# Spare products of a projection stage in the general PSUM banks, in turn with the projections

## Chip, cores, metric

The kernel runs on one core of a Trainium2 chip. The metric is device time in microseconds (us) of one execution, the median of several runs. A second kernel, the change, computes the same thing with the same instructions in another order.

## What is computed

Two layers of a hybrid block work on 512 image tokens and 256 context tokens of width 1024. Cut to one layer:

```
h  = rms_norm(x) * (1 + scale) + shift          # also hc, of the context
(a_qkv, a_z, a_beta, a_alpha, b_q, b_kv, b_z, c_qkv, c_z, merge) = split(h @ w_in)
y_a = gated_head_rmsnorm(bidir_delta(short_conv(a_qkv), ...), a_z)   # 4 heads, chunks of 64
y_b = window_attention(b_q, b_kv, ...) * silu(b_z)
y_c = retention_out(bidir_retention(c_qkv), c_z)
out = (sigmoid(merge)[0] * (y_a @ w_br[0]) + sigmoid(merge)[1] * (y_b @ w_br[1])
       + sigmoid(merge)[2] * (y_c @ w_br[2])) @ w_o
x   = x + gate * out                            # context likewise, but not in the last layer
```

Branch A is a gated delta rule: in every chunk a unit lower triangular matrix is inverted (`triangular_solve` in the reference), then a chain of states runs over the chunks in both directions. Nothing of the `z` columns and of the `merge` columns is needed until the branches end.

## The kernel before

Every product with `w_in` is made in blocks of 128 columns, named by what they are: `aq0` to `aq3`, `ak0`.., `av0`.. are the projections of branch A, `az`, `bz`, `cz` the gates of the three branches, `m0_0` to `m2_7` the merge gates. A weight block is loaded (`wr`), cast by ScalarE to `wh` and its remainder taken by GpSimd as `wl`; `prod` (L305) then does 24 matmuls of 512 columns into a `px` bank for the image tokens and, in layer 0 only, 24 of 256 columns into a `pc` bank for the context (`hh`, `hl` are the two parts of `h`). PSUM has 2 `px` banks, 1 `pc` bank and 5 general ones (`pg`, `gps` at L252).

The A heads are worked in two pairs. For a pair, `delta_proj` makes six projections, each followed by a short convolution: one tap on ScalarE, the others as `scalar_tensor_tensor` on VectorE (L285), then turned to tokens by TensorE (`to_tok`, L602). `delta_mats` makes the chunk matrices with small matmuls in `pg` banks and VectorE's L285 and L288. `delta_inv` inverts the 32x32 blocks on VectorE: transposes (L733, L735), 62 short L288 operations, transposes back (L747, L748), then copies of the blocks on VectorE (L763) and ScalarE (L766, 12 of 32x192 elements). `levels` (L790) combines the blocks on TensorE; its first matmul waits for all copies. `delta_chain` is the chain over the chunks.

What nobody needs soon fills TensorE in the meantime: the generator `aside` (L1211) makes the spare products, the z and merge gates, one per step. ScalarE writes `tanh` of the bank into `kept` (L282 is the helper of every activation); for a z block VectorE also multiplies `kept` with the bank (L285), so that a z bank comes free only behind VectorE. Then ScalarE's queue stores `kept` in DRAM. `weave` at L1297 to L1302 sets the stages of a layer, and `FILL[l]` how many spare products stand in each: beside the projections of the second pair (with the matrices and inverse of the first), first chain, second pair's matrices, second inverse, second chain, each attention step, and ahead of the second token product `tokproj(w1)`. `BACK` says behind the how-many-last spare product the levels may begin on TensorE.

The order on each engine is fixed when the program is built: a scheduler with priorities (`hi`) sorts the instructions. An engine does them in that order, so a wait of one holds up all behind it.

```
        for nm in ms[0:6] + z("a") + ms[6:8] + z("b") + ms[8:12] + z("c") + ms[12:]:
            px, pc = self.pblk(l, nm, not last)
            self.asides.append(self.last)
```

Of the kernel before, what the change touches and what calls it, by code (L numbers as in the profile page):

```python
# [9 lines left out]
F32 = mybir.dt.float32  # L10
F32R = mybir.dt.float32r
BF16 = mybir.dt.bfloat16
AF = mybir.ActivationFunctionType
# [4 lines left out]
D, SEQ, CTX, DEPTH = 1024, 512, 256, 2  # L18
# [14 lines left out]
C1 = 3  # L33
AH = 2
BG = (0, 2)
FILL = ((5, 4, 2, 7, 5, 1, 1), (6, 3, 3, 9, 5, 1, 2))
BACK = ((2, 3), (2, 2))

NAMES = (["aq%d" % i for i in range(4)] + ["ak%d" % i for i in range(4)]
# [5 lines left out]
BLK = {n: i for i, n in enumerate(NAMES)}  # L45
# [117 lines left out]
class Builder:  # L163
# [142 lines left out]
    def prod(self, ps, w, acts, sl, ks=None):  # L306
        hi, lo = w
        n = len(acts)
        ks = ks or range(n)
        for k in ks:  # L310
            self.mm(ps, hi[k], acts[k][0].r[:, sl], start=(k == 0), stop=False)
            self.mm(ps, hi[k], acts[k][1].r[:, sl], start=False, stop=False)
        for k in ks:
            self.last = self.mm(ps, lo[k], acts[k][0].r[:, sl], start=False, stop=(k == n - 1)).ins.name

    def proj(self, dram, acts, ctx, w=None):
        w = w or self.weight(dram, len(acts))
        px = self.px.tile([128, 512], F32, name="px")
        self.prod(px, w, acts, slice(0, SEQ))
        pc = None  # L320
        if ctx:
            pc = self.pc.tile([128, 512], F32, name="pc")[:, 0:CTX]
            self.prod(pc, w, acts, slice(SEQ, TOK))
        return px, pc

# [27 lines left out]
                self.prod(ps[i], w, self.hs, PART[i], range(k0[i], k))  # L353
                k0[i] = k

    def pblk(self, l, name, ctx, w=None):
# [9 lines left out]
        return self.proj(self.a["wblk"][l, BLK[name]], self.hs, ctx, w)  # L366


    def ada_head(self):
# [347 lines left out]
    def delta_inv(self, st, back):  # L717
# [37 lines left out]
        for d in range(2):  # L755
            wsrc, tsrc = (Z, M) if d == 0 else (M, Z)

            own, other = (0, 2) if d == 0 else (3, 1)
            for hh, h in enumerate(st.heads):
                W[h, d] = self.alloc()  # L760
                nc.gpsimd.memset(W[h, d].f, 0.0)
                for q in range(4):
                    made.append(nc.vector.tensor_copy(blk(W[h, d], q), lane(wsrc, q, d, hh)))  # L763
                for q, t, c in ((own, Q, 32 * (own % 2)), (own + 1 - 2 * d, Q, 32 * (1 - own % 2)), (other, T, 0)):
                    made.append(self.act(six(t.f)[32 * q:32 * q + 32, hh, :, c:c + 32],
                                         lane(tsrc, q, d, hh), AF.Copy))  # L766
                yield
        self.free_inv()
        yield from self.levels(st, W, T, Q, made, self.asides[-back])
        self.free(T, Q, *st.U.values())  # L770

    def levels(self, st, W, T, Q, made, behind):
# [440 lines left out]
    def aside(self, l, last):  # L1213
        nc = self.nc
        n = SEQ if last else TOK
        self.kept = {}
        z = lambda b: ["%sz%d" % (b, i) for i in range(4)]
        ms = ["m%d_%d" % (r, d) for r in range(3) for d in range(8)]
        for nm in ms[0:6] + z("a") + ms[6:8] + z("b") + ms[8:12] + z("c") + ms[12:]:
            px, pc = self.pblk(l, nm, not last)  # L1220
            self.asides.append(self.last)
            t = self.fp.tile([128, TOK], F32, name="kept")
            for ps, sl in ((px, slice(0, SEQ)), (pc, slice(SEQ, TOK)))[:1 if last else 2]:
                self.act(t[:, sl], ps, AF.Tanh, scale=0.5)
                if nm[1] == "z":
                    self.stt(t[:, sl], t[:, sl], 1.0, ps, ALU.add, ALU.mult)
            g = self.dp.tile([128, n], F32, name="%s_%d" % (nm, l))
            nc.scalar.dma_start(g, t[:, 0:n])
            self.kept[nm] = g
            yield  # L1230
# [9 lines left out]
    def layer(self, l, xs, rs, mod, vec, row, ada):  # L1240
# [12 lines left out]
        self.asides = []  # L1253
        self.fill = self.aside(l, last)
        self.mods = self.ada(ada) if ada else iter(())
        F = FILL[l]
# [37 lines left out]
        self.delta_gates(l, ba, row)  # L1294
        for _ in p0:
            pass
        weave((seq(self.delta_mats(l, last, st[0]), self.delta_inv(st[0], BACK[l][0])), 45),  # L1297
              (self.delta_proj(l, 1, vec, last, st[1]), 6), fill(F[0]))
        weave((self.hi(self.delta_chain(l, last, st[0])), 6), fill(F[1]))
        weave((self.hi(self.delta_mats(l, last, st[1])), 4), fill(F[2]))  # L1300
        weave((self.hi(self.delta_inv(st[1], BACK[l][1])), 43), fill(F[3]))
# [157 lines left out]
def seq(*gens):  # L1459
    for g in gens:  # L1460
        yield from g


def weave(*tasks):

    live = [[0.0, i, g, n] for i, (g, n) in enumerate(tasks)]
    while live:
        t = min(live)
        try:
            next(t[2])  # L1470
            t[0] += 1.0 / t[3]
        except StopIteration:
            live.remove(t)
# [22 lines left out]
```

## Time and profile before

| what | value |
|---|---|
| median of 3 runs | 1822.45 us (1821.61 to 1828.53) |
| the profiled execution, its own time | 1822.54 us |
| its span | 1820.7 us |
| mean granted clock of TensorE | 0.978 |
| TensorE busy | 1716.5 us, 94% of the span |
| VectorE busy | 1051.9 us, 58% |
| ScalarE busy | 843.8 us, 46% |
| GpSimd busy | 591.9 us, 33% |

PE is TensorE, PEld its weight loads, DVE VectorE, ACT ScalarE, POOL GpSimd, SP SyncE. A row of a timeline gives the start, the duration, the engine, the line, the operation and the tiles it writes and reads; in square brackets at its end stands how long the engine was idle just before and what released it. A granted clock of 1.00 is 2.4 GHz, 0.5 is 1.2 GHz.

### The profile page before, as it was taken

Reading aid. Unit: us, or ns where it says so; the run is one execution under the profiler, and the core shown is the slowest. Engines: PE = TensorE matmul, PEld = TensorE weight load, DVE = VectorE, ACT = ScalarE, POOL = GpSimd, SP = SyncE. Lnnn points to the kernel's source line nnn. Section 1 sums busy time; section 2 is a strip of 40 time slices with the busy share of each in tenths; the row PEclk is TensorE's granted clock in tenths of the full one; section 3 lists DMA queues with packets and bytes.
Section 4 is the critical chain, followed back from the end, with each engine's and each line's share of the span. In section 5 each row is a group of like instructions: output and inputs, shape, how many; then the busy total and the mean of one; then the engine's idle time right before and its main releaser. Section 6 shows DMA issues by size and latency. Waiting matters only on the chain. (4 is left out here: it accounts for less than half of the span.)

```text
span 1820.7 us, 30653 instructions
## 1 busy us (share of the span) xinstructions
PE 1716.5 (94%) x11574; PEld 1457.0 (80%) x11574; DVE 1051.9 (58%) x2531; ACT 843.8 (46%) x2018; POOL 591.9 (33%) x739
## 2 busy tenths in 40 slices
PE   7999999899999999999999899889799999999997
PEld 4788888788877778988888688678688777888786
DVE  4668758732564553346563647957925657445653
ACT  6565546343544544222233556365444655433244
POOL 2322422312312214121453614432333322322553
PEclk9999999999999999999999899989999999999998
DMA  8211211322244233014453112212233332212542
GB/s 310 80 35 65 85 33 62 110 77 105 81 140 154 96 127 132 33 53 145 134 176 112 59 41 76 93 36 67 96 111 122 116 105 80 90 53 82 170 160 70
DMA packets 73748, 180.67 MB, mean 99 GB/s; under 512 B 8832, under 2 KB 16384, under 8 KB 73600
## 3 DMA queue, kind: packets, MB, share of 16 engines
q1 hardware_dynamic: 62144, 154.07, 26.1%
q10 hardware_dynamic: 11456, 24.65, 3.6%
q8 instruction: 91, 1.49, 0.3%
q14 instruction: 57, 0.47, 0.1%
HBM read 150.89 MB, written 27.79 MB: 98 GB/s over the span
## 5 line engine op out<-in xcount | busy, mean ns | idle before, releaser
L291 POOL TENSOR_TENSOR wl<-wr,wh 128x256 fp32r<-128x256 f32 x640 | 505.0, 818 | 1058.3 <-ACT wh L282 805.6
L261 PE MATMUL px<-hh,wh 128*128 128x512 f32 (+1 forms) x1088 | 433.8, 403 | 24.5 <-DVE kept L285 11.8
L261 PE MATMUL px<-hl,wh 128*128 128x512 f32 (+1 forms) x1088 | 431.9, 399 | 3.4 <-DVE hl L285 1.9
L261 PE MATMUL px<-hh,wl 128*128 128x512 f32 (+1 forms) x1088 | 286.9, 394 | 0.0
L282 ACT ACTIVATE wh<-wr 128x1024 fp32r<-128x1024 f32 (+1 forms) x184 | 174.3, 947 | 229.5 <-PE pc L261 109.3
L288 DVE TENSOR_TENSOR t<-t,t 128x512 f32<-128x512 f32 (+21 forms) x411 | 252.9, 616 | 42.3 <-ACT t L282 29.7
L261 PEld LDWEIGHTS px<-hh,wh 128*128 128x128 f32 x1088 | 209.3, 193 | 69.8 <-DVE kept L285 14.3
L282 ACT ACTIVATE t<-t 32x192 f32<-32x192 f32 (+10 forms) x314 | 168.2, 548 | 194.4 <-DVE t L285 124.6
L261 PEld LDWEIGHTS px<-hl,wh 128*128 128x128 f32 x1088 | 210.3, 193 | 44.1 <-DVE hl L285 6.8
L261 PE MATMUL pg<-t,t 128*128 128x128 f32 (+2 forms) x1616 | 231.3, 285 | 11.4 <-DVE t L288 11.0
L261 PEld LDWEIGHTS pg<-t,t 128*128 128x128 f32 x1616 | 206.6, 191 | 34.0 <-issue 11.6
L261 PEld LDWEIGHTS px<-hh,wl 128*128 128x128 f32 x1088 | 198.7, 191 | 37.6 <-issue 2.0
L261 PE MATMUL pc<-hh,wh 128*128 128x256 f32 x696 | 176.4, 288 | 9.9 <-DVE kept L285 5.7
L261 PE MATMUL pc<-hl,wh 128*128 128x256 f32 x696 | 177.6, 290 | 1.9 <-DVE hl L285 1.9
L261 PEld LDWEIGHTS pc<-hh,wh 128*128 128x128 f32 x696 | 134.4, 193 | 15.7 <-DVE kept L285 6.6
L261 PEld LDWEIGHTS pc<-hl,wh 128*128 128x128 f32 x696 | 134.9, 194 | 7.1 <-DVE hl L285 3.2
L282 ACT ACTIVATE t<-pg 128x128 f32<-128x128 f32 (+4 forms) x216 | 77.6, 383 | 109.7 <-PE pg L408 37.0
L261 PE MATMUL px<-t,wh 128*128 128x512 f32 x384 | 101.5, 402 | 4.2 <-DVE t L285 4.1
L261 PE MATMUL pc<-hh,wl 128*128 128x256 f32 x696 | 103.8, 289 | 0.0
L282 ACT ACTIVATE t<-px 128x128 f32<-128x128 f32 (+2 forms) x120 | 54.7, 465 | 101.8 <-PE px L261 94.6
L261 PEld LDWEIGHTS pc<-hh,wl 128*128 128x128 f32 x696 | 92.7, 196 | 0.9 <-issue 0.8
L261 PE MATMUL px<-t,hh 128*128 128x272 f32 (+1 forms) x384 | 86.6, 313 | 1.3 <-POOL t L291 1.0
(191 smaller groups left out, 2320.8 us busy)
## 6 DMA issues: line engine op xcount, KB each, us to landing
wr<-wblk SPq DMA_DIRECT2D x120, 512.0 KB, 3.3
t<-wada SPq DMA_DIRECT2D x48, 384.0 KB, 4.6
wr<-wbr SPq DMA_DIRECT2D x48, 256.0 KB, 2.7
m<-kept ACTq DMA_DIRECT2D x24, 384.0 KB, 2.3
t<-m SPq DMA_DIRECT2D x24, 384.0 KB, 3.6
wr<-wout SPq DMA_DIRECT2D x16, 512.0 KB, 3.3
t<-wada SPq DMA_DIRECT2D x24, 256.0 KB, 4.8
m<-kept ACTq DMA_DIRECT2D x24, 256.0 KB, 2.0
```

What stands on the lines that cost most here:

```text
L261: return self.nc.tensor.matmul(out, lhsT=lhsT, rhs=rhs, start=start, stop=stop)
L282: return self.nc.scalar.activation(out, in_, func, **k)
L288: self.nc.vector.tensor_tensor(out=out, in0=in0, in1=in1, op=op)
L291: self.nc.gpsimd.tensor_tensor(out=out, in0=in0, in1=in1, op=op)
```

## The change

It has four parts. The numbers of spare products per stage change (`FILL`). Their order changes: in layer 0 and 1 the first 5 and 6 are merge gates, then two `az`, then merge gates up to the second inverse, then the other two `az`, the `bz` and the `cz`; so the second pair's matrices and inverse have merge gates alone. In the projection stage (`self.behind`) a spare product takes `pg` banks, and a projection may be issued only behind the last spare product made so far, so that the two alternate on TensorE. In `delta_inv` ScalarE's copies are issued behind the tanh of an earlier spare product.

```
@@ -33,7 +33,7 @@
 C1 = 3
 AH = 2
 BG = (0, 2)
-FILL = ((5, 4, 2, 7, 5, 1, 1), (6, 3, 3, 9, 5, 1, 2))
+FILL = ((5, 2, 4, 7, 6, 1, 0), (6, 2, 4, 9, 6, 1, 1))
 BACK = ((2, 3), (2, 2))
 
 NAMES = (["aq%d" % i for i in range(4)] + ["ak%d" % i for i in range(4)]
@@ -311,15 +311,16 @@
             self.mm(ps, hi[k], acts[k][0].r[:, sl], start=(k == 0), stop=False)
             self.mm(ps, hi[k], acts[k][1].r[:, sl], start=False, stop=False)
         for k in ks:
-            self.last = self.mm(ps, lo[k], acts[k][0].r[:, sl], start=False, stop=(k == n - 1)).ins.name
-
-    def proj(self, dram, acts, ctx, w=None):
+            self.end = self.mm(ps, lo[k], acts[k][0].r[:, sl], start=False, stop=(k == n - 1)).ins
+            self.last = self.end.name
+
+    def proj(self, dram, acts, ctx, w=None, other=False):
         w = w or self.weight(dram, len(acts))
-        px = self.px.tile([128, 512], F32, name="px")
+        px = self.gps() if other else self.px.tile([128, 512], F32, name="px")
         self.prod(px, w, acts, slice(0, SEQ))
         pc = None
         if ctx:
-            pc = self.pc.tile([128, 512], F32, name="pc")[:, 0:CTX]
+            pc = self.gps(CTX) if other else self.pc.tile([128, 512], F32, name="pc")[:, 0:CTX]
             self.prod(pc, w, acts, slice(SEQ, TOK))
         return px, pc
 
@@ -353,7 +354,7 @@
                 self.prod(ps[i], w, self.hs, PART[i], range(k0[i], k))
                 k0[i] = k
 
-    def pblk(self, l, name, ctx, w=None):
+    def pblk(self, l, name, ctx, w=None, other=False):
         if l == 0 and name in self.begun:
             b = self.begun[name]
             self.advance(b, KB)
@@ -363,7 +364,10 @@
                 self.prod(pc, w, self.hs, slice(SEQ, TOK))
             self.free(*held)
             return px, pc
-        return self.proj(self.a["wblk"][l, BLK[name]], self.hs, ctx, w)
+        if self.behind and not other and self.asides:
+            with self.tc.issue_after(self.asides[-1][2]):
+                return self.proj(self.a["wblk"][l, BLK[name]], self.hs, ctx, w)
+        return self.proj(self.a["wblk"][l, BLK[name]], self.hs, ctx, w, other)
 
 
     def ada_head(self):
@@ -762,11 +766,12 @@
                 for q in range(4):
                     made.append(nc.vector.tensor_copy(blk(W[h, d], q), lane(wsrc, q, d, hh)))
                 for q, t, c in ((own, Q, 32 * (own % 2)), (own + 1 - 2 * d, Q, 32 * (1 - own % 2)), (other, T, 0)):
-                    made.append(self.act(six(t.f)[32 * q:32 * q + 32, hh, :, c:c + 32],
-                                         lane(tsrc, q, d, hh), AF.Copy))
+                    with self.tc.issue_after(self.asides[-back][1]):
+                        made.append(self.act(six(t.f)[32 * q:32 * q + 32, hh, :, c:c + 32],
+                                             lane(tsrc, q, d, hh), AF.Copy))
                 yield
         self.free_inv()
-        yield from self.levels(st, W, T, Q, made, self.asides[-back])
+        yield from self.levels(st, W, T, Q, made, self.asides[-back][0])
         self.free(T, Q, *st.U.values())
 
     def levels(self, st, W, T, Q, made, behind):
@@ -1216,14 +1221,16 @@
         self.kept = {}
         z = lambda b: ["%sz%d" % (b, i) for i in range(4)]
         ms = ["m%d_%d" % (r, d) for r in range(3) for d in range(8)]
-        for nm in ms[0:6] + z("a") + ms[6:8] + z("b") + ms[8:12] + z("c") + ms[12:]:
-            px, pc = self.pblk(l, nm, not last)
-            self.asides.append(self.last)
+        a, b = FILL[l][0], sum(FILL[l][0:4]) - 2
+        for nm in ms[0:a] + z("a")[0:2] + ms[a:b] + z("a")[2:4] + z("b") + z("c") + ms[b:]:
+            px, pc = self.pblk(l, nm, not last, None, self.behind)
+            pe = self.last
             t = self.fp.tile([128, TOK], F32, name="kept")
             for ps, sl in ((px, slice(0, SEQ)), (pc, slice(SEQ, TOK)))[:1 if last else 2]:
-                self.act(t[:, sl], ps, AF.Tanh, scale=0.5)
+                th = self.act(t[:, sl], ps, AF.Tanh, scale=0.5)
                 if nm[1] == "z":
                     self.stt(t[:, sl], t[:, sl], 1.0, ps, ALU.add, ALU.mult)
+            self.asides.append((pe, th.ins, self.end))
             g = self.dp.tile([128, n], F32, name="%s_%d" % (nm, l))
             nc.scalar.dma_start(g, t[:, 0:n])
             self.kept[nm] = g
@@ -1250,7 +1257,7 @@
         for k in range(KB):
             self.tap("hh%d_%d" % (l, k), self.hs[k][0].f)
             self.tap("hl%d_%d" % (l, k), self.hs[k][1].f)
-        self.asides = []
+        self.asides, self.behind = [], False
         self.fill = self.aside(l, last)
         self.mods = self.ada(ada) if ada else iter(())
         F = FILL[l]
@@ -1294,8 +1301,10 @@
         self.delta_gates(l, ba, row)
         for _ in p0:
             pass
+        self.behind = True
         weave((seq(self.delta_mats(l, last, st[0]), self.delta_inv(st[0], BACK[l][0])), 45),
               (self.delta_proj(l, 1, vec, last, st[1]), 6), fill(F[0]))
+        self.behind = False
         weave((self.hi(self.delta_chain(l, last, st[0])), 6), fill(F[1]))
         weave((self.hi(self.delta_mats(l, last, st[1])), 4), fill(F[2]))
         weave((self.hi(self.delta_inv(st[1], BACK[l][1])), 43), fill(F[3]))
```

Three places of the new order follow. The number behind a tile's name tells one buffer's use from another's.

TensorE in layer 0's projection stage, where the product of `av2` begins (`px_1747`). The tiles 1670 and 1695 are the banks of spare product `m0_1`, for the image and for the context. Before:

```order
727 L261 MATMUL px_1670<-hh6_97,wl_1663 128x512 [waits Pool_49]
728 L261 MATMUL px_1670<-hh7_99,wl_1663 128x512
729 L261 MATMUL px_1747<-hh0_85,wh_1739 128x512 [waits Activation_49]
730 L261 MATMUL px_1747<-hl0_86,wh_1739 128x512
731 L261 MATMUL px_1747<-hh1_87,wh_1739 128x512
```

Now:

```order
751 L261 MATMUL pg_1695<-hh5_95,wl_1663 128x256
752 L261 MATMUL pg_1695<-hh6_97,wl_1663 128x256
753 L261 MATMUL pg_1695<-hh7_99,wl_1663 128x256
754 L261 MATMUL px_1747<-hh0_85,wh_1739 128x512 [waits Activation_49]
755 L261 MATMUL px_1747<-hl0_86,wh_1739 128x512
```

`m0_1` has moved from `px` and `pc` to two general banks, and its context half now stands ahead of `av2` instead of behind it.

ScalarE in layer 0's second inverse: the copies are the rows with 32x6x32 elements, the tanh rows write `kept`. `px_3482` is a bank of `bz0`, the first z product of the stage. Before:

```order
385 L282 ACTIVATE kept_3450<-pc_3425 128x256 [waits PE_49]
386 L1228 DMA m0_7_0_3453<-kept_3450 128x768 [waits Activation_49]
387 L282 ACTIVATE t195_3858<-t190_3377 32x6x32 [waits DVE_49]
388 L282 ACTIVATE t195_3858<-t190_3377 32x6x32 x3
389 L282 ACTIVATE t194_3857<-t190_3377 32x6x32
390 L282 ACTIVATE t195_3858<-t191_3378 32x6x32 [waits DVE_49]
391 L282 ACTIVATE t195_3858<-t191_3378 32x6x32 x3
392 L282 ACTIVATE t194_3857<-t191_3378 32x6x32 x2
393 L282 ACTIVATE t194_3857<-t190_3377 32x6x32
394 L282 ACTIVATE kept_3532<-px_3482 128x512 [waits DMAHW0_49,PE_49]
```

Now:

```order
400 L282 ACTIVATE kept_3680<-pc_3655 128x256 [waits PE_49]
401 L282 ACTIVATE t195_3846<-t191_3374 32x6x32 [waits DVE_49]
402 L282 ACTIVATE t195_3846<-t191_3374 32x6x32 x2
403 L282 ACTIVATE t194_3845<-t191_3374 32x6x32
404 L282 ACTIVATE t195_3846<-t191_3374 32x6x32
405 L282 ACTIVATE t194_3845<-t191_3374 32x6x32
406 L1235 DMA m1_4_0_3683<-kept_3680 128x768 [waits DMAHW2_49,Activation_49]
407 L282 ACTIVATE kept_3756<-px_3706 128x512 [waits DMAHW7_49,PE_49]
408 L282 ACTIVATE wh_3867<-wr_3866 128x1024 [waits DMAHW0_49,PE_49,Pool_49]
409 L282 ACTIVATE kept_3756<-pc_3731 128x256 [waits PE_49]
410 L282 ACTIVATE t195_3846<-t190_3373 32x6x32 x4
411 L282 ACTIVATE t194_3845<-t190_3373 32x6x32 x2
```

The twelve copies have moved from between two tanhs early in the stage to its end, six behind the context tanh of `m1_4` and six behind that of `m1_5`, the last whole product ahead of the levels.

ScalarE in layer 1's second inverse, where a product has no context half. Before, the copies stand behind the tanh of `bz2` (`px_13066`), five products ahead of the levels:

```order
1253 L282 ACTIVATE wh_13156<-wr_13155 128x1024 [waits PE_49,DMAHW2_49,Activation_49,Pool_49]
1254 L282 ACTIVATE kept_13091<-px_13066 128x512 [waits DMAHW3_49,PE_49]
1255 L1228 DMA bz2_1_13094<-kept_13091 128x512 [waits DVE_49]
1256 L282 ACTIVATE t650_13338<-t645_12941 32x6x32 [waits DVE_49]
1257 L282 ACTIVATE t650_13338<-t645_12941 32x6x32 x3
1258 L282 ACTIVATE t649_13337<-t645_12941 32x6x32
```

Now:

```order
1267 L282 ACTIVATE kept_13229<-px_13204 128x512 [waits DMAHW1_49,PE_49]
1268 L1235 DMA m1_7_1_13231<-kept_13229 128x512 [waits Activation_49]
1269 L282 ACTIVATE wh_13371<-wr_13370 128x1024 [waits DMAHW4_49,PE_49,Pool_49]
1270 L282 ACTIVATE kept_13277<-px_13252 128x512 [waits DMAHW3_49,PE_49]
1271 L282 ACTIVATE t650_13332<-t646_12940 32x6x32 [waits DVE_49]
1272 L282 ACTIVATE t650_13332<-t645_12939 32x6x32 x2
1273 L282 ACTIVATE t650_13332<-t646_12940 32x6x32
```

The copies have moved behind the tanh of `m2_0` (`px_13252`); one product, `m2_1`, stands between it and the levels.

## Rows read from the trace of the kernel before

**Rows 1.** The page: busy time, share and instructions of each engine.

```profile
PE 1716.5 (94%) x11574; PEld 1457.0 (80%) x11574; DVE 1051.9 (58%) x2531; ACT 843.8 (46%) x2018; POOL 591.9 (33%) x739
```

**Rows 2.** Waits of TensorE: us in total, times, longest us.

```profile
PE px L261 <- DVE kept L285: 11.8, 6, 4.7
...
PE px L261 <- ACT kept L282: 3.7, 2, 2.6
```

**Rows 3.** Windows: length, busy PE, PEld, DVE, ACT, POOL, granted clock, DMA, GB/s.

```profile
160.00:200.00 40.00, 36.87 (x218) 32.34 (x218) 38.70 (x84) 15.35 (x34) 13.03 (x16) 1.00 0.21 73
...
1176.00:1207.00 31.00, 20.08 (x88) 16.18 (x86) 25.32 (x54) 17.26 (x35) 12.44 (x17) 0.81 0.13 48
...
1318.00:1325.00 7.00, 4.79 (x11) 3.79 (x12) 1.58 (x5) 2.98 (x4) 5.58 (x8) 0.51 0.40 115
```

**Rows 4.** Timeline of ScalarE, layer 0's projection stage.

```profile
159.88 2.13 ACT L282 ACTIVATE t<-t 32x192 f32<-32x192 f32 x4 [1.58 <-DVE t L288]
162.03 0.60 ACT L282 ACTIVATE kept<-px 128x512 f32<-128x512 f32 x1
```

**Rows 5.** Timeline of TensorE there: the start of av2.

```profile
162.68 0.50 PE L261 MATMUL px<-hh,wh 128*128 128x512 f32 x1 [2.65 <-ACT kept L282]
```

**Rows 6.** Timeline of ScalarE, layer 0's second inverse.

```profile
343.69 6.30 ACT L282 ACTIVATE t<-t 32x192 f32<-32x192 f32 x12 [9.78 <-DVE t L747]
350.01 0.60 ACT L282 ACTIVATE kept<-px 128x512 f32<-128x512 f32 x1
```

**Rows 7.** Timeline of TensorE, layer 0: end of the projections, second inverse.

```profile
236.13 1.51 PE L602 MATMUL pg<-c,t 128*128 128x128 f32 x6 [3.43 <-DVE t L285]
...
352.46 0.58 PE L261 MATMUL pc<-hh,wh 128*128 128x256 f32 x1 [5.21 <-DVE kept L285]
...
355.58 0.28 PE L261 MATMUL pc<-hh,wh 128*128 128x256 f32 x1
355.70 0.28 PE L261 MATMUL pc<-hl,wh 128*128 128x256 f32 x1
```

**Rows 8.** Timeline of ScalarE, end of layer 1's projection stage.

```profile
1188.80 3.45 ACT L282 ACTIVATE t<-t 32x192 f32<-32x192 f32 x6 [1.31 <-DVE t L748]
1192.28 0.69 ACT L282 ACTIVATE t<-px,vec 128x512 f32<-128x512 f32 x1
1192.99 2.84 ACT L282 ACTIVATE t<-t 32x192 f32<-32x192 f32 x5
```

**Rows 9.** Timeline of TensorE there: av3, its context half, the last transposes.

```profile
1183.38 0.77 PE L261 MATMUL px<-hh,wh 128*128 128x512 f32 x1 [6.66 <-DVE t L285]
...
1191.28 0.28 PE L261 MATMUL pc<-hh,wh 128*128 128x256 f32 x1
...
1204.04 1.52 PE L602 MATMUL pg<-c,t 128*128 128x128 f32 x6 [4.26 <-DVE t L285]
```

**Rows 10.** Timeline of TensorE, layer 1's second inverse; L790 begins the levels.

```profile
1269.85 0.50 PE L261 MATMUL px<-hh,wh 128*128 128x512 f32 x1 [2.13 <-DVE kept L285]
...
1277.03 0.39 PE L261 MATMUL px<-hh,wh 128*128 128x512 f32 x1
...
1282.47 0.39 PE L261 MATMUL px<-hh,wh 128*128 128x512 f32 x1
...
1320.21 0.80 PE L261 MATMUL px<-hh,wh 128*128 128x512 f32 x1 [4.66 <-DVE kept L285]
...
1338.96 1.02 PE L790 MATMUL pg<-t,t 32*32 32x32 f32 x96
```

**Rows 11.** Timeline of ScalarE there: the copies.

```profile
1311.92 5.95 ACT L282 ACTIVATE t<-t 32x192 f32<-32x192 f32 x12 [7.57 <-DVE t L747]
```

**Rows 12.** Timeline of VectorE there: the last 15 of its copies.

```profile
1314.34 4.56 DVE L763 COPY t<-t 32x192 f32<-32x192 f32 x15 [0.26 <-issue]
```

**Rows 13.** Timeline of TensorE, layer 1's second token product.

```profile
1570.53 0.44 PE L261 MATMUL px<-t,hh 128*128 128x384 f32 x1 [0.47 <-POOL t L291]
1571.53 0.62 PE L261 MATMUL px<-t,hh 128*128 128x384 f32 x2 [0.56 <-POOL t L291]
```

More of the change, by code (lines that the diff above doesn't have):

```diff
@@ L313, in prod, with proj @@
         for k in ks:
-            self.last = self.mm(ps, lo[k], acts[k][0].r[:, sl], start=False, stop=(k == n - 1)).ins.name
-    def proj(self, dram, acts, ctx, w=None):
+            self.end = self.mm(ps, lo[k], acts[k][0].r[:, sl], start=False, stop=(k == n - 1)).ins
+            self.last = self.end.name
+    def proj(self, dram, acts, ctx, w=None, other=False):
         w = w or self.weight(dram, len(acts))
-        px = self.px.tile([128, 512], F32, name="px")
+        px = self.gps() if other else self.px.tile([128, 512], F32, name="px")
         self.prod(px, w, acts, slice(0, SEQ))
@@ L321, in proj @@
         if ctx:
-            pc = self.pc.tile([128, 512], F32, name="pc")[:, 0:CTX]
+            pc = self.gps(CTX) if other else self.pc.tile([128, 512], F32, name="pc")[:, 0:CTX]
             self.prod(pc, w, acts, slice(SEQ, TOK))
@@ L354, in advance, with pblk @@
                 k0[i] = k
-    def pblk(self, l, name, ctx, w=None):
+    def pblk(self, l, name, ctx, w=None, other=False):
         if l == 0 and name in self.begun:
@@ L365, in pblk @@
             return px, pc
-        return self.proj(self.a["wblk"][l, BLK[name]], self.hs, ctx, w)
+        if self.behind and not other and self.asides:
+            with self.tc.issue_after(self.asides[-1][2]):
+                return self.proj(self.a["wblk"][l, BLK[name]], self.hs, ctx, w)
+        return self.proj(self.a["wblk"][l, BLK[name]], self.hs, ctx, w, other)
     def ada_head(self):
@@ L764, in delta_inv @@
                 for q, t, c in ((own, Q, 32 * (own % 2)), (own + 1 - 2 * d, Q, 32 * (1 - own % 2)), (other, T, 0)):
-                    made.append(self.act(six(t.f)[32 * q:32 * q + 32, hh, :, c:c + 32],
-                                         lane(tsrc, q, d, hh), AF.Copy))
+                    with self.tc.issue_after(self.asides[-back][1]):
+                        made.append(self.act(six(t.f)[32 * q:32 * q + 32, hh, :, c:c + 32],
+                                             lane(tsrc, q, d, hh), AF.Copy))
                 yield
         self.free_inv()
-        yield from self.levels(st, W, T, Q, made, self.asides[-back])
+        yield from self.levels(st, W, T, Q, made, self.asides[-back][0])
         self.free(T, Q, *st.U.values())
@@ L1218, in aside @@
         ms = ["m%d_%d" % (r, d) for r in range(3) for d in range(8)]
-        for nm in ms[0:6] + z("a") + ms[6:8] + z("b") + ms[8:12] + z("c") + ms[12:]:
-            px, pc = self.pblk(l, nm, not last)
-            self.asides.append(self.last)
+        a, b = FILL[l][0], sum(FILL[l][0:4]) - 2
+        for nm in ms[0:a] + z("a")[0:2] + ms[a:b] + z("a")[2:4] + z("b") + z("c") + ms[b:]:
+            px, pc = self.pblk(l, nm, not last, None, self.behind)
+            pe = self.last
             t = self.fp.tile([128, TOK], F32, name="kept")
             for ps, sl in ((px, slice(0, SEQ)), (pc, slice(SEQ, TOK)))[:1 if last else 2]:
-                self.act(t[:, sl], ps, AF.Tanh, scale=0.5)
+                th = self.act(t[:, sl], ps, AF.Tanh, scale=0.5)
                 if nm[1] == "z":
                     self.stt(t[:, sl], t[:, sl], 1.0, ps, ALU.add, ALU.mult)
+            self.asides.append((pe, th.ins, self.end))
             g = self.dp.tile([128, n], F32, name="%s_%d" % (nm, l))
@@ L1252, in layer @@
             self.tap("hl%d_%d" % (l, k), self.hs[k][1].f)
-        self.asides = []
+        self.asides, self.behind = [], False
         self.fill = self.aside(l, last)
```

4 lines of the change are left out of this document (3 added, 1 removed).

## Prediction

> **What bounds the kernel now.** I read the table of busy times first, then that of TensorE's waits. TensorE is busy 1716.5 us, 94% of the span [rows 1], so a change that only reorders can win no more than its idle time and the time at half clock behind the longer idle stretches. The reader is to see in [rows 2] which waits have to do with the spare products: TensorE waiting for a `px` bank that VectorE has yet to read into `kept` (11.8 us in 6 waits) and for one that ScalarE's tanh still holds (3.7 us in 2). Next come the windows: between 160 and 200 us VectorE is busy 38.70 of 40 us at full granted clock; between 1176 and 1207 us, and between 1318 and 1325 us, the granted clock is 0.81 and 0.51 [rows 3]. The timelines then show each place.
>
> In layer 0's projection stage, av2 starts 2.65 us late [rows 5] because the tanh that frees its bank stands on ScalarE behind four 32x192 activations that wait for VectorE [rows 4]. In layer 0's second inverse, ScalarE does twelve copies in one piece, 343.69 to 349.99 us, and only then a tanh [rows 6]; the `pc` of a z product waits 5.21 us for the VectorE read behind that tanh [rows 7]. In layer 1's second inverse, five starts of a product wait for VectorE's `kept` reads, from 2.13 us at the first to 4.66 us at the last [rows 10], because those reads stand between the inverse's own instructions, which fill VectorE.
>
> **The sum, part by part.** It is made against the profiled execution, 1822.54 us (span 1820.7 plus 1.8 around it), which is 0.1 us above the median of the three runs.
>
> *Layer 0, projections alternating with spares in the general banks.* av2's `px` bank was last held by a projection two steps earlier, no longer by m0_1. The 2.65 us wait [rows 5] goes: **-2.7 us**. The 3.43 us wait at 236.13 us [rows 7] stays, since it waits for the last convolution on VectorE, and the order there does not change. Queued behind it are only the inverse's levels.
>
> *Layer 0, first chain and second pair's matrices (4, 2 products become 2, 4).* TensorE has less filler in the chain. The trace has no row of that. Bounds: nothing, if the chain's engines keep up as now, and one wait like the 2.65 us of [rows 5]. I take **+1.0 us**, nearer to nothing, because the same number of products stands between the two ends.
>
> *Layer 0, second inverse.* Merge gates need only a tanh, so no bank waits for VectorE, and half of the copies now follow the `pc` tanh of the last whole product before the levels, the other half that of the product before it. The 5.21 us go. So does the half clock behind them: 14 matmuls start between 352.46 and 355.58 us, 3.12 us, where at the spacing of the next two (0.12 us) they would take 1.7 [rows 7], a loss of 1.4 us. Next late is the first matmul of the levels: it needs the last six copies, half of 6.30 us [rows 6], behind a 0.36 us tanh, while TensorE has nine matmuls of 0.227 us (5.44 us for 24, [rows 10]), 2.0 us, to do. That is a wait of 3.15 + 0.36 - 2.04, so 1.5 us. Together **-5.1 us**; bounds -6.6 (no new wait) and -0.3 (a wait for the whole 6.30 us).
>
> *Layer 1, projections.* TensorE no longer waits 6.66 us for av3's bank [rows 9]. But the stage does not end sooner for that. ScalarE does six copies from 1188.80 us, then av3's first tap at 1192.28 and five more copies at 1192.99, ahead of the tap of its `pc` [rows 8]; they wait for VectorE's inverse, not for TensorE, and their order is the same in the change. The transposes at 1204.04 us [rows 9] are released by VectorE after these. The 6.66 us and the 2.5 us lost in av3 at half clock (7.90 us from its start to the next product, 5.44 at full) come back in the wait ahead of 1204.04: **0**, bounds -3 (what VectorE might interleave better; nearest is the 2.5 us) and +2.6 (one wait as in [rows 5]).
>
> *Layer 1, second inverse, the largest term.* The ten products between the matrices and the levels change from z products and gates mixed to merge gates alone. Their banks come free by a tanh of some 0.6 us right behind the product. The five waits go, 11.6 of the 11.8 us in [rows 2]. The half clock behind the first and the last goes too: 7.18 us from 1269.85 to 1277.03 us against 5.44 for the next product, 1.7 us, and 18.75 us from 1320.21 to 1338.96 for three products against 16.3, 2.4 us [rows 10]. Is TensorE then still covered by VectorE? Ten products of 5.44 us from 1267.72 us (2.13 before 1269.85) end at 1322.1 us. VectorE's copies end at 1318.90 us even today [rows 12], and lose `kept` reads ahead of them, so VectorE is not late. ScalarE's twelve copies now follow the tanh of the last product but one: 0.6 + 5.95 us [rows 11] against the 5.44 us of the last product, a wait of some 1.2 us in front of the levels. Behind them on ScalarE stand one weight cast and one tanh, of which neither is needed at once. **-14.5 us**; bounds -15.7 and -9.7 (the whole 5.95 us waited for).
>
> *z products moved to second chain and attention.* Their VectorE reads now stand where that engine has room. The trace shows no such row in a second chain. Bounds: nothing, and 2.1 us in each layer, as the first wait in [rows 10]; I take **0**, the nearer, as the first chain runs with z products today.
>
> *Tails.* One spare product less stands right before the second token product in each layer, one more ahead of the attention. In layer 1 that product already waits 0.47 and 0.56 us for GpSimd's splits [rows 13]. Arriving earlier by up to one product, it would wait up to 5.4 us more, or nothing if the splits shift too. I take **+2.5 us** for both layers.
>
> Sum: -2.7 + 1.0 - 5.1 + 0 - 14.5 + 0 + 2.5 = -18.8 us, **1803.7 us**.
>
> **Rivals.**
>
> *The waits come back at the levels.* If the copies are released later than I read, both inverses wait for all twelve, 6.30 and 5.95 us in place of 1.5 and 1.2, and the tails and matrices take their upper ends (5.4 and 2.65 us): 9.6 + 2.9 + 1.7 = 14.2 us given back, **1817.9 us**. For it: twelve copies in one piece are what ScalarE does today [rows 6, 11]. Against: each engine's new order has the copies behind an early tanh.
>
> *The general banks run short: slower.* In both projection stages, eleven spare products now take general banks, which the matrices and the transposes turn over too. If a product's tanh is held up on ScalarE as m0_1's was [rows 4], the next user of its bank waits 2.65 us [rows 5]. It decides from eight of the eleven on (18.8 / 2.65 = 7.1); all eleven cost 29.2 us, **1832.9 us**. Against it: five general banks stand behind each other, and the wait in [rows 5] arose with two.
>
> *The clock drops in the projection stages.* Today the granted clock is 1.00 in the 40 us around the 2.65 us wait, and 0.81 where waits of 6.66 and 4.26 us stand [rows 3, 9]. Were it 0.81 through both stages (some 76 us to 236 us, some 70 us to 1204 us), matmuls would take 19% of 146 us longer, 28 us: **1831.7 us**. The Trainium skill, "TensorE: Matmul & The Clock Gate", section "A second HAM failure mode: psum-queue depth-cycling", says that passing matmul groups through a cycle of banks can bring short idle stretches between them and make the clock go up and down, which speaks against this change. By that rule the time would be this rival's; here the trace does not agree so far, as the short waits around 160 us left the clock at 1.00.
>
> **How the numbers follow.** The forecast has a chance of 0.68; its own range, from the bounds of its terms, is 1797 to 1813. The waits at the levels have 0.20, the general banks 0.09, the clock 0.03. 0.5% is 9.1 us, about what a measurement of this kernel can tell from no change. Faster than 1813.4: the forecast, nearly whole, and a third of the first rival, where only one inverse waits: 0.73. Within: the rest of that rival, and a few of the general banks' cases where half of the products wait: 0.17. Slower: 0.10. The range 1796 to 1817 leaves out the slower cases and a part of the first rival.
>
> **What would show it.** In the profile of the changed kernel, TensorE's waits for `px` and `pc` with VectorE's `kept` as releaser should fall from 17 us (11.8 and 5.21) to under 3; av2 in layer 0 should start without a wait; layer 1's ten products from 1267 us should run without idle time at a granted clock of 1.00; two waits of 1 to 2 us should stand before the levels; the transposes near 1204 us should wait 10 us or more in one piece. I am wrong if the levels wait 6 us, if general-bank waits for ScalarE's `kept` show in the projection stages, or if layer 1's inverse ends on VectorE.

## The result, and the profile after

The changed kernel takes 1810.97 us (median of 4 runs, 1805.86 to 1814.13), the kernel before 1822.03 us in the runs beside it: a ratio of 0.9931, 95% interval 0.9914 to 0.9947, some 11 us less (0.7%). The profiled execution is the fastest of the four, 1805.86 us with a span of 1803.7.

The page of the changed kernel, busy times (before: [rows 1]):

```profile
PE 1704.5 (95%) x11574; PEld 1449.5 (80%) x11574; DVE 1060.1 (59%) x2531; ACT 844.6 (47%) x2018; POOL 595.5 (33%) x739
```

TensorE's waits in it: us in total, times, longest us (before: [rows 2]):

```profile
PE px L261 <- ACT wh L282: 10.7, 2, 10.4
PE pg L606 <- DVE t L285: 8.8, 5, 4.3
PE px L261 <- ACT kept L282: 6.3, 1, 6.3
...
PE pg L795 <- ACT t L282: 4.8, 7, 1.4
```

No row with VectorE's `kept` as releaser is left; before, these waits made 17 us in sum. What came in their place is in TensorE's timeline (the idle time before a row stands in brackets), from layer 0's levels to layer 1's second levels:

```profile
367.14 1.02 PE L795 MATMUL pg<-t,t 32*32 32x32 f32 x96 [1.42 <-ACT t L282]
...
1123.24 0.77 PE L261 MATMUL pg<-hh,wh 128*128 128x512 f32 x1 [2.98 <-DVE t L285]
...
1192.26 0.80 PE L261 MATMUL px<-hh,wh 128*128 128x512 f32 x1 [10.36 <-ACT wh L282]
...
1310.73 0.79 PE L261 MATMUL px<-hh,wh 128*128 128x512 f32 x1 [6.28 <-ACT kept L282]
1326.03 1.02 PE L795 MATMUL pg<-t,t 32*32 32x32 f32 x96 [1.37 <-ACT t L282]
```

Three of these five rows were forecast in size: 1.5 us and 1.2 us before the two levels, and 10 us in layer 1's projection stage, though there ahead of the last transposes. A wait for a general bank was among the rivals. The 6.28 us at 1310.73 were in neither. The queue of SyncE in that stretch, which issues the loads (the duration of a row is the stretch its issues span):

```profile
1265.69 20.81 SPq L300 DMA_DIRECT2D wr<-wblk  x5
1304.71 0.33 SPq L1243 DMA_DIRECT2D t<-az  x1
1305.20 25.08 SPq L300 DMA_DIRECT2D wr<-wblk  x6
```

and ScalarE there:

```profile
1309.14 1.06 ACT L282 ACTIVATE wh<-wr 128x1024 fp32r<-128x1024 f32 x1 [14.93 <-DMA wr<-wblk]
1310.10 0.58 ACT L282 ACTIVATE kept<-px 128x512 f32<-128x512 f32 x1
```

The read-back of the gate az0 from DRAM (L1243) stands on SyncE's queue between the weight loads of m1_7 and m2_0. It fills a buffer that the inverse on VectorE still uses, so it is issued only at 1304.71, when VectorE's last short operation is done, and every later weight load waits with it. ScalarE waits 14.93 us for the next weights, and the tanh that would free a `px` bank is queued behind that cast. In the windows (length, busy PE, PEld, DVE, ACT, POOL, granted clock, DMA, GB/s) the DMA share is nought before, and TensorE runs at half clock behind the wait:

```profile
1300.00:1305.00 5.00, 4.46 (x20) 3.37 (x18) 4.49 (x16) 0.00 (x0) 0.00 (x0) 1.00 0.00 0
1305.00:1310.00 5.00, 0.00 (x0) 0.00 (x0) 4.95 (x11) 0.86 (x1) 0.00 (x0) 0.98 0.76 256
1310.00:1315.00 5.00, 4.27 (x10) 3.40 (x11) 4.93 (x8) 2.22 (x4) 4.73 (x7) 0.50 0.34 127
```

### The profile page after: what moved, and what is told of

It reads as the page before. It is cut to its first block, busy times and chain, and to the rows that moved or that the text cites. A ratio compares the mean times of both kernels' runs of the same rounds, so it can differ in the third digit from the quotient of the medians.

```text
span 1803.7 us, 30670 instructions
## 1 busy us (share of the span) xinstructions
PE 1704.5 (95%) x11574; PEld 1449.5 (80%) x11574; DVE 1060.1 (59%) x2531; ACT 844.6 (47%) x2018; POOL 595.5 (33%) x739
## 5 line engine op out<-in xcount | busy, mean ns | idle before, releaser
L261 PE MATMUL px<-hh,wh 128*128 128x512 f32 (+1 forms) x1000 | 393.0, 397 | 19.4 <-ACT wh L282 10.4
L261 PE MATMUL px<-hl,wh 128*128 128x512 f32 (+1 forms) x1000 | 393.4, 396 | 4.4 <-DVE hl L285 3.0
L261 PE MATMUL px<-hh,wl 128*128 128x512 f32 (+1 forms) x1000 | 263.2, 393 | 0.0
L261 PE MATMUL pg<-t,t 128*128 128x128 f32 (+2 forms) x1616 | 230.3, 285 | 11.6 <-DVE t L288 11.3
L261 PEld LDWEIGHTS px<-hh,wh 128*128 128x128 f32 x1000 | 190.4, 191 | 58.4 <-ACT wh L282 11.0
L261 PEld LDWEIGHTS px<-hl,wh 128*128 128x128 f32 x1000 | 191.4, 191 | 41.9 <-DVE hl L285 7.5
L261 PEld LDWEIGHTS px<-hh,wl 128*128 128x128 f32 x1000 | 181.4, 190 | 33.2 <-issue 1.2
L261 PE MATMUL pc<-hh,wh 128*128 128x256 f32 x656 | 165.6, 287 | 3.7 <-DVE t L285 3.7
L261 PE MATMUL pc<-hl,wh 128*128 128x256 f32 x656 | 166.7, 289 | 2.0 <-DVE hl L285 2.0
L261 PEld LDWEIGHTS pc<-hh,wh 128*128 128x128 f32 x656 | 125.9, 192 | 8.4 <-DVE t L285 4.1
L261 PEld LDWEIGHTS pc<-hl,wh 128*128 128x128 f32 x656 | 126.2, 192 | 6.7 <-DVE hl L285 3.2
```

The lines of the kernel that those rows point to most:

```text
L261: return self.nc.tensor.matmul(out, lhsT=lhsT, rhs=rhs, start=start, stop=stop)
```

## The experiments

All runs compute the same thing. They were made on several chips, each beside runs of the kernel before on the same chip (medians 1821.9 to 1823.0 us), so across chips the ratios are to be compared. The table has, for each, the median, the ratio to the runs of the kernel before on the same chip with its interval, and for four stages of the profiled execution the length and TensorE's idle time in it, in us. The stages are read from TensorE's timeline: P is from a layer's first transposes to tokens (L602, now L606) to its first levels (L790, now L795), I from the first levels to the second.

| kernel | median | ratio | P, layer 0 | I, layer 0 | P, layer 1 | I, layer 1 |
|---|---|---|---|---|---|---|
| before | 1822.0 | 1 | 162.5, 9.4 | 134.7, 6.4 | 155.7, 13.9 | 131.8, 13.8 |
| the change | 1811.0 | 0.9931 [0.9914, 0.9947] | 160.0, 7.4 | 132.0, 2.1 | 158.1, 15.6 | 124.9, 9.4 |
| after_again | 1812.4 | 0.9943 [0.9925, 0.9961] | 162.0, 7.9 | 132.1, 2.2 | 157.4, 16.6 | 125.6, 10.1 |
| order_alone | 1825.9 | 1.0017 [1.0005, 1.0029] | 165.5, 11.6 | 139.9, 10.2 | 156.9, 14.6 | 129.4, 14.7 |
| tie_alone | 1825.4 | 1.0016 [1.0002, 1.0030] | 164.8, 10.7 | 140.3, 7.5 | 155.7, 14.8 | 132.0, 15.4 |
| banks_alone | 1820.7 | 0.9993 [0.9980, 1.0007] | 160.4, 7.9 | 136.1, 6.6 | 158.6, 16.0 | 132.0, 14.2 |
| no_tie | 1826.1 | 1.0016 [1.0003, 1.0029] | 160.6, 7.9 | 140.1, 10.1 | 158.2, 16.8 | 129.9, 15.0 |
| no_banks | 1809.3 | 0.9924 [0.9908, 0.9941] | 162.5, 10.3 | 132.5, 2.3 | 156.1, 14.4 | 124.5, 9.5 |
| no_turns | 1806.3 | 0.9908 [0.9889, 0.9927] | 161.1, 7.2 | 131.3, 2.1 | 154.2, 15.1 | 123.8, 9.5 |
| az0_late | 1804.6 | 0.9900 [0.9880, 0.9919] | 162.0, 7.9 | 132.1, 2.3 | 157.4, 16.6 | 117.0, 4.4 |
| before_late | 1821.7 | 0.9998 [0.9984, 1.0012] | 163.1, 10.0 | 136.5, 6.5 | 155.6, 14.9 | 130.7, 14.2 |
| late_no_banks | 1807.0 | 0.9907 [0.9885, 0.9929] | 163.1, 10.1 | 131.0, 2.1 | 156.8, 15.4 | 118.3, 4.6 |
| late_layer0_banks | 1801.9 | 0.9883 [0.9863, 0.9904] | 162.0, 8.0 | 131.2, 2.2 | 155.7, 13.4 | 117.8, 4.5 |
| late_no_turns | 1800.0 | 0.9875 [0.9853, 0.9896] | 161.0, 7.3 | 131.3, 2.1 | 154.9, 15.7 | 117.2, 4.6 |

### The changed kernel once more

> The changed kernel once more, as the yardstick of the runs beside it. Theory: 9 to 13 us under the kernel before (ratio 0.993 to 0.995). In its profile TensorE waits again about 6.3 us on a kept copy in layer 1's second inverse, straight behind a stretch in which SyncE's queue stands at the read-back of az0, and about 3 us for a general bank in layer 1's projection stage. Rival, that those waits were chance of one execution: one of the two is under 1 us here.

1812.4 us. Both waits are there again: 3.00 us for the general bank, 6.45 us on the kept copy, behind an az0 row at 1306.60. They belong to the program, not to one execution. The 2 us between the two executions in the first column are a wait of 4.9 in place of 4.3 us, and half clock behind waits.

### az0's read-back behind the weight loads

```
-            nc.sync.dma_start(w, dram)
+            self.wdma = nc.sync.dma_start(w, dram).ins
...
+        if nm == "az0":
+            with self.tc.issue_after(self.wdma):
+                self.nc.sync.dma_start(s.f[:, 0:n], self.kept[nm])
```

> The changed kernel with the read-back of az0 put on SyncE's queue behind the weight load of the last product of the second chain, so that no weight load stands behind its wait for an inverse buffer. Theory (the queue is what holds the products up in layer 1's second inverse): the wait of 6.3 us on a kept copy and the half clock behind it (48 products in 13.9 us, where 48 at full clock take 11.0) go, the weight loads of the stage stand in one row on the queue, and the levels start 6 to 9 us sooner; 6 to 9 us under the changed kernel, about 1802 to 1805 us. Rival A (the products wait for ScalarE's own work, the casts and the copies): a wait of at least 4 us on ScalarE stays in the stage, and the time is within 2 us of the changed kernel. Rival B (the inverse on VectorE ends the stage anyhow): the wait goes from the products to the levels, 5 us or more before the first of them, time within 2 us.

1804.6 us, 7.9 under the changed kernel on the same chip, as the theory has it. The edit moves az0's read-back in both layers. The order on TensorE, VectorE, ScalarE and GpSimd is the same, only SyncE's queue differs, and in layer 1 its weight loads stand in one row:

```profile
1259.89 63.76 SPq L300 DMA_DIRECT2D wr<-wblk  x12
1328.84 0.33 SPq L1247 DMA_DIRECT2D t<-az  x1
```

The wait on the kept copy is gone, and the stage is 8.6 us shorter than in after_again. Rival A falls with that. Rival B shows a little: the levels wait 2.43 us instead of 1.37, for ScalarE's copies, and these now wait for VectorE's transposes (last section).

```profile
1319.40 1.02 PE L795 MATMUL pg<-t,t 32*32 32x32 f32 x96 [2.43 <-ACT t L282]
```

### The same in the kernel before

The same edit in the kernel before, as a control.

> The kernel before with the read-back of az0 behind the weight load of the last product of the second chain, as in the run az0_late. Theory (in the kernel before the products of layer 1's second inverse were held by VectorE's kept sums and by the copies on ScalarE, so the held queue had no price): within 2 us of the kernel before. Rival (the queue cost the kernel before as much): 5 us or more under it, which would make the wait no part of what the change turned up.

1821.7 us, no change. In the kernel before no load was late for az0's sake. Its row waits 3.1 us for VectorE and is issued at 1310.67, and the next load goes out only at 1321.85. That load waits not for az0 but for GpSimd, which begins to split the weights in the load's buffer at 1319.03, after 11.89 us without work (`wr` has two buffers). The rows are of SyncE's waits from 1255 to 1345 us, of its queue, and of GpSimd's timeline:

```profile
SPq L1236 <- DVE t L288: 3.1, 1, 3.1
...
1310.67 0.33 SPq L1236 DMA_DIRECT2D t<-az  x1
1321.85 20.46 SPq L300 DMA_DIRECT2D wr<-wblk  x5
...
1319.03 5.59 POOL L291 TENSOR_TENSOR wl<-wr,wh 128x256 fp32r<-128x256 f32 x8 [11.89 <-ACT wh L282]
```

In the changed kernel the same row holds the queue for 18.2 us (SyncE's waits in the same stretch):

```profile
SPq L1243 <- DVE t L288: 18.2, 1, 18.2
```

The queue became a price only when the products got faster. The change also put az0's row one load earlier, behind 93 weight loads in place of 94; what this alone is worth was not tried.

### The order alone

The change without general banks, turns and tie: `self.behind` stays `False`, and ScalarE's copies stand free.

```
-                    with self.tc.issue_after(self.asides[-back][1]):
-                        made.append(self.act(six(t.f)[32 * q:32 * q + 32, hh, :, c:c + 32],
-                                             lane(tsrc, q, d, hh), AF.Copy))
+                    made.append(self.act(six(t.f)[32 * q:32 * q + 32, hh, :, c:c + 32],
+                                         lane(tsrc, q, d, hh), AF.Copy))
...
-        self.behind = True
+        self.behind = False
```

> The new numbers of products per stage and the new order of names alone: the products of the projection stage stay in the px and pc banks and are not turned with the projections, the copies are not tied to a tanh. Theory (most of the gain is that the inverse stages hold merge gates alone, which need no VectorE): layer 1's inverse stage keeps its gain of some 7 us and layer 0's inverse some 3 us of it, the projection stages read as in the kernel before; 7 to 11 us under the kernel before, with the waits of px on kept from VectorE under 3 us in sum. Rival (the banks carry the gain): within 3 us of the kernel before. Second rival (the order pays only with the tie): a wait of 4 us or more on ScalarE's copies stands before a level, and the time is within 4 us of the kernel before.

1825.9 us, over the kernel before: the theory falls, and the second rival is right in kind. VectorE's `kept` is gone from the waits, yet TensorE waits 9.33 us in layer 0's inverse and 13.05 in layer 1's:

```profile
1328.17 0.79 PE L261 MATMUL px<-hh,wh 128*128 128x512 f32 x1 [13.05 <-ACT kept L282]
```

ScalarE's rows say why. Its twelve copies stand ahead of a weight cast and a tanh, and wait there for VectorE's transpose:

```profile
1320.37 6.19 ACT L282 ACTIVATE t<-t 32x192 f32<-32x192 f32 x12 [15.49 <-DVE t L751]
1326.58 1.06 ACT L282 ACTIVATE wh<-wr 128x1024 fp32r<-128x1024 f32 x1
1327.54 0.58 ACT L282 ACTIVATE kept<-px 128x512 f32<-128x512 f32 x1
```

### The tie taken out of the change

Only the first half of the edit above.

> The changed kernel without the tie of ScalarE's copies to a tanh. Theory (seen in the run of the order alone: free to move, the copies stand on ScalarE ahead of a weight cast and a tanh, wait there for VectorE's transpose, and hold the products): waits of 8 to 14 us of px or pc on a kept copy come back straight before the copies in the second inverse of each layer; 10 to 18 us over the changed kernel, 1822 to 1830 us. Rival (the loss of that run came from the missing banks, which shift when products and inverse meet): waits under 4 us there, and within 4 us of the changed kernel.

1826.1 us, with 9.30 and 13.06 us of the same waits: all of the gain is lost, with the general banks in place.

```profile
PE px L261 <- ACT kept L282: 13.1, 1, 13.1
...
PE pc L261 <- ACT kept L282: 9.3, 1, 9.3
```

### The tie alone

The change with `self.behind = False`, the `FILL` and the line of names of the kernel before.

> The tie of ScalarE's copies to a tanh alone: numbers of products, order of names and banks as in the kernel before. Theory (the order takes VectorE out of the products' way, the tie takes the copies out of it, and each is worth little alone because the other hold comes last at nearly the same time): the waits on kept sums from VectorE stay, in layer 1's second inverse 12 us in sum as before; within 4 us of the kernel before. Rival (the tie is the whole gain, the order nothing): 8 us or more under the kernel before.

1825.4 us, within the 4 us. VectorE's `kept` sums stay the releasers:

```profile
PE px L261 <- DVE kept L285: 11.7, 5, 4.1
...
PE pc L261 <- DVE kept L285: 5.2, 2, 4.7
```

The loss lies in layer 0's inverse stage, 5.6 us longer than before: 9 more matmuls stand ahead of the levels there (249 into `px`, 240 before; 2 us), the levels wait 1.52 us, and the granted clock is 0.96 in place of 0.99.

So order and tie pay only as a pair: alone each costs some 3 us against the kernel before (the intervals just leave out no change), together (no_banks) they give 13. While z products stand in the inverse, the bank waits for VectorE whether the copies are tied or not; with merge gates there and free copies, it waits for the copies.

### The general banks alone

The change with the `FILL` and names of the kernel before, and without the tie.

> The general banks and the turns with the projections alone: the numbers of products per stage and the order of names are those of the kernel before, the copies are not tied. Theory: layer 0's projection stage gains about 2.5 us, layer 1's loses about 2.4 us by its wait for a general bank, and the rest reads as in the kernel before: within 3 us of it. Rival (the banks carry the gain): 8 us or more under the kernel before. Second rival (the banks do harm by themselves): 4 us or more over it.

1820.7 us: no difference that can be measured, as the theory had it. Layer 0's projection stage is 2.1 us shorter, layer 1's 2.9 longer, with 2.84 us of wait for a general bank.

### The general banks taken out

`self.behind = False` in the change; order and tie stay.

> The changed kernel without the general banks and without the turns with the projections: order and tie stay. Theory (order and tie together make the gain, the banks give some 2.5 us in layer 0's projection stage and take about as much in layer 1's): within 3 us of the changed kernel, and 8 to 13 us under the kernel before; layer 1's projection stage has no wait of 3 us for a general bank. Rival (the banks are part of what the order needs): 5 us or more over the changed kernel, with px waits for VectorE's sums back in layer 0's projection stage and new waits in the inverses.

1809.3 us, the whole gain without the part that names the change. Layer 1's projection stage is 1.3 to 2.0 us shorter than in the two profiles of the change.

### The turns taken out

The spare products stay in the general banks, the projections are free to move.

```
-        if self.behind and not other and self.asides:
+        if False:
```

> The changed kernel with the spare products of the projection stage in the general banks, but the projections no longer held behind the spare product before them. Theory (the bank is what takes the wait away, the turns only keep the order that the costs give anyway): within 3 us of the changed kernel. Rival (without the turns TensorE meets two projections in a row, whose px banks VectorE has not emptied): 4 us or more over it, with waits of px on VectorE's sums of 2 us or more in a projection stage.

1806.3 us, some 6 under after_again (by ratio 0.9908 against 0.9943, whose intervals just touch): the theory asked for within 3, so the turns seem to cost something. Against the first runs of the change, 0.9931, the intervals overlap. The 2.98 us wait is cut to 1.02:

```profile
1126.35 0.47 PE L261 MATMUL pg<-hh,wh 128*128 128x512 f32 x1 [1.02 <-DVE t L285]
```

and layer 1's projection stage (154.2 and 154.9 us in the two runs without turns) is the shortest of all. Most of layer 1's wait came from the turns, not from the banks: with them m0_1 has to come where its bank is still being read by VectorE.

### Put together

az0's read-back late, and in turn: no general banks; general banks and turns in layer 0 alone (`self.behind = l == 0`); general banks without turns.

> Order and tie, no general banks and no turns, and az0's read-back behind the last weight load of the second chain. Theory: what the read-back costs is there with and without the banks, so 6 to 9 us under the run without banks: 1800 to 1804 us, the wait of 5.8 us on a kept copy at 1308.6 gone. Rival: within 3 us of it, because another wait takes its place.

1807.0 us, 2.3 under no_banks (3.1 by the ratios): in time it missed the 6 to 9 us and lies at the rival's 3 us, and the two intervals overlap. In its place it did what the theory says: the wait of 5.8 us is gone and the stage 6.2 us shorter (124.5 to 118.3), with 2.44 us before the levels. Some 1.5 us came back before that stage and 1.6 behind it, where the compute engines have the same order. The clock does not explain it: the granted clock of the two profiled executions is 0.981 and 0.982. The cause stays open.

> General banks and turns in layer 0 alone, with az0's read-back behind the last weight load of the second chain. Theory (the banks give 2.5 us in layer 0 and take 2.4 in layer 1): 1800 to 1803 us, 2 to 4 under the run az0_late. Rival (the banks in layer 1 cost nothing, the clock of one execution made it look so): within 1.5 us of the run az0_late.

1801.9 us, 2.7 under az0_late (3.1 by the ratios), as expected, but the intervals of the two overlap.

> The changed kernel without the turns, and with az0's read-back behind the last weight load of the second chain. Theory (the two effects lie in different stages and add): 5 to 9 us under the run without turns, 1797 to 1801 us. Rival: the two don't add, and it is within 2 us of the run az0_late, 1804.6.

1800.0 us, 6.2 under no_turns, as the theory had it. That the effects add is seen in the stages, 154.9 and 117.2 us side by side; in time the interval overlaps those of no_turns and az0_late. This version has the lowest median here, 0.9875 of the kernel before (0.9853 to 0.9896), and it beats the change as well (the intervals don't meet).

## Why the prediction was right, and where not

The forecast was 1803.7 us against 1822.5; the median came to 1811.0, inside the range, on the side that had the chance of 0.73. Against its own yardstick, the profiled execution, the sum of -18.8 us met -16.7. That closeness is partly luck, as the terms show (spans; change less before):

- *Layer 0, projections, -2.7.* The mechanism is right: av2 no longer waits [rows 5]; its wait stands in all six profiles without general banks there (2.64 to 2.66 us) and in none of the eight with them. The stage is 2.5 us shorter in this execution, 0.5 in the repeated one; 160.0 to 162.0 us in the eight, 162.5 to 165.5 in the six. Part of the gain comes back where the forecast had it stay: the 3.43 us wait for the last convolution [rows 7] is 4.31 us here and 4.3 to 4.9 in the others of the eight.
- *Layer 0, chain, matrices and second inverse, -4.1 in sum.* TensorE's idle time fell by 4.3 us (6.4 to 2.1), and the new wait before the levels is 1.42 us where 1.5 was forecast. The stage is 2.7 us shorter; it now also holds 9 more matmuls ahead of its end (249 into `px`, 240 before), 2 us at 0.227 us each.
- *Layer 1, projections, 0.* It became +2.4: a general bank was waited for once, 2.98 us at 1123.24, not eight times, and for VectorE's read of it, not for the tanh on ScalarE that the rival had. The step that failed is that the edit was priced at av3 alone, and not at the point where a turn makes a product come before its bank is free. As foreseen, av3's 6.66 us [rows 9] were not won: they went into the 10.36 us at 1192.26. The releaser was not the one I named; it is az0's weight cast, queued on ScalarE behind the twelve copies:

```profile
1183.93 3.23 ACT L282 ACTIVATE t<-t 32x192 f32<-32x192 f32 x6 [0.36 <-ACT r L282]
1187.19 0.69 ACT L282 ACTIVATE t<-px,vec 128x512 f32<-128x512 f32 x1
1187.90 3.22 ACT L282 ACTIVATE t<-t 32x192 f32<-32x192 f32 x6
1191.15 1.06 ACT L282 ACTIVATE wh<-wr 128x1024 fp32r<-128x1024 f32 x1
```

- *Layer 1, second inverse, -14.5.* It became -6.9. **This is the step that failed**: "Their banks come free by a tanh of some 0.6 us right behind the product." The tanh was there, but stood behind a weight cast on ScalarE whose weights stood behind az0's read-back on SyncE. I followed the products through TensorE, ScalarE and VectorE and did not follow the loads through SyncE's queue, where az0's row, one load earlier than before, came to wait 18.2 us instead of 3.1. The rows of the new order show the like of it, a weight cast that waits for a DMA ahead of a tanh (1269 and 1270), but not when that DMA is issued. With that one read-back moved the stage is 117.0 us, 14.8 less than the 131.8 before: the term as forecast, with two sizes that make up for each other, 2.43 us before the levels where 1.2 was forecast, and a granted clock of 1.00 in the whole stage (0.95 before).
- *Tails, +2.5.* Not seen. From layer 0's second levels to layer 1's first transposes the two profiles of the change take 675.9 and 676.3 us, the one before 677.9; from layer 1's second levels to the end of TensorE's work 468.7 and 470.4, before 472.8. The other runs have 676.2 to 680.4 and 469.1 to 473.3: nothing that stands out from single executions. The last stretch goes with the granted clock in it: 0.99 in the change's profile, 0.98 in the repeated run, 0.97 before.

In the profiled execution the 11.6 us by which the four stages fell short (0.2, 1.4, 2.4 and 7.6) were nearly made up by the tails, -2.0 and -4.1 us where +2.5 was forecast, and by 1.2 us ahead of the first stage, where the instructions are the same. The median of four does not have that luck, and is 7 us off.

Of the rivals, the waits at the levels did not come (1.42 and 1.37 us), but only thanks to the tie; without it the copies cost 9.3 and 13.1 us, more than that rival had. The rival of the clock came true in a small part. Over layer 0's whole projection stage the granted clock is 0.99 before and after (1.00 again in the window from 160 to 200 us, now with no idle time). Over layer 1's it is 0.96 before, 0.94 in the change and 0.95 in the repeated run, but 0.97 without the turns, far from 0.81 throughout. Of the 3.2 to 3.9 us by which that stage is shorter in no_turns, TensorE's idle time makes up 0.5 to 1.5; the rest goes with the clock. In the window of [rows 3] it is 0.78, near the 0.81 there.

```profile
160.00:200.00 40.00, 40.00 (x238) 35.55 (x237) 38.77 (x84) 15.59 (x34) 15.21 (x19) 1.00 0.24 83
1176.00:1207.00 31.00, 18.96 (x342) 15.68 (x341) 21.07 (x43) 17.75 (x37) 10.82 (x13) 0.78 0.12 42
```

Two numbers of the forecast do not follow from their own terms, though the sum does not rest on them. The clock's price of 28 us is too low: TensorE was busy 153.0 and 141.9 us in the two stages at 0.99 and 0.96, so at 0.81 they would be some 60 us longer, an estimate from these figures. And the bounds of the terms, added up, reach from 1794.5 to 1824.7 us, not from 1797 to 1813.

## What to carry to other kernels

When a reordering makes one stage faster, follow every queue that feeds it, the loads' queue too: a load that waits for a buffer holds all loads behind it, and that costs nothing until the work behind it gets quick. Two holds that end at nearly the same time must be taken away together; tried singly, each of them looks worthless or worse. And a forced alternation is worth a test against leaving the order to the costs, with the banks kept.

## What was not expected of the hardware

VectorE's inverse is slower when GpSimd works. Its last 16 short operations before the transposes are the same instructions in both kernels. In the changed kernel GpSimd stands idle then (no weights had come), in az0_late it splits two weight blocks. The changed kernel's VectorE:

```profile
1299.61 5.03 DVE L288 TENSOR_TENSOR t<-t,t 128x192 f32<-128x192 f32 x16
1304.67 1.25 DVE L751 STREAM_TRANSPOSE t<-t 128x1024 f32<-128x1024 f32 x1
```

az0_late's VectorE:

```profile
1301.79 8.10 DVE L288 TENSOR_TENSOR t<-t,t 128x192 f32<-128x192 f32 x16
1309.92 1.25 DVE L751 STREAM_TRANSPOSE t<-t 128x1024 f32<-128x1024 f32 x1
...
1313.07 5.94 DVE L767 COPY t<-t 32x192 f32<-32x192 f32 x16
```

and its GpSimd:

```profile
1300.79 3.19 POOL L291 TENSOR_TENSOR wl<-wr,wh 128x256 fp32r<-128x256 f32 x4 [1.94 <-ACT wh L282]
1306.23 2.87 POOL L291 TENSOR_TENSOR wl<-wr,wh 128x256 fp32r<-128x256 f32 x4 [2.25 <-ACT wh L282]
```

5.03 us become 8.10. Seven of the 16 operations are slowed, all while a split runs, and six of them by the same amount, whatever their own length: one of 0.357 us takes 0.778, one of 0.251 takes 0.671, 0.42 more each (the seventh takes 0.55 more); those that meet none take what they took. The first levels begin at the same time in az0_late and after_again (1202.4), yet VectorE's transposes start at 1309.92 against 1306.56. So a little of what the loads gave is taken back, some 1 us: ScalarE's copies wait for the transposes, and the levels start at 1319.40, right behind the last of these copies (VectorE's own end at 1319.01).

```profile
1313.18 3.86 ACT L282 ACTIVATE t<-t 32x192 f32<-32x192 f32 x7 [1.01 <-DVE t L752]
...
1316.95 2.40 ACT L282 ACTIVATE t<-t 32x192 f32<-32x192 f32 x5
```

The Trainium skill, "SBUF — State Buffer", section "Who interferes with whom", says that a VectorE instruction with two inputs in SBUF and a GpSimd instruction that reads SBUF take turns at a shared pair of ports, one waiting until the other is done. The trace agrees: both operations here have two inputs in SBUF, and an addition of 0.42 us that does not depend on the operation's own length is what waiting in turn would give.
